# A two-layer SSD, attention and convolution trunk on one core: paired 128-column diagonal products, a padded decay contraction, dt weights side by side, and shorter chains in layer 0

## The chip, the cores and the metric

The kernel runs on one core of a Trainium2 chip. The metric is the device time of one execution in microseconds. The time before is 939.8 us, the median of three runs (937.92 to 940.81).

## The reference

The reference is a trunk of two layers on 512 tokens of width 1024, in float32. Each layer computes `x + RMSNorm_post(mixer(RMSNorm_pre(x)))`.

Layer 0 projects the normalised input once (`w_in`, 7200 columns) and splits it into gates `z`, an SSD branch (`xbc`, `dt`), and a forgetting-attention branch (`q`, `k`, `v`, `f`). The SSD branch is Mamba-2 in chunks of 128 tokens, with 16 heads of 64 columns in 4 groups:

```python
cs = jnp.cumsum(da, axis=2)                       # within a chunk of 128
decay = jnp.exp(jnp.where(causal, seg, -jnp.inf)) # seg[l, s] = cs[l] - cs[s]
cb = jnp.einsum('bclgn,bcsgn->bclsg', cc, bc)
y_diag = jnp.einsum('bclsgr,bcsgrp->bclgrp', cb[..., None] * decay, xd)
...
y_off = jnp.einsum('bclgn,bcgrpn->bclgrp', cc, h_in) * jnp.exp(cs)[..., None]
return (y_diag + y_off).reshape(bsz, s, g, r, p)
```

Its result is gated by `silu(z)`, normalised per group, joined with the gated output of the attention branch (16 heads, causal, with a decay in the logits), and multiplied by `w_out` (2048 x 1024). Layer 1 is a causal Conformer module: a projection to 6144 columns, a gated linear unit, a depthwise convolution of width 31, LayerNorm, a second gate, and an output projection (2048 x 1024).

## The kernel before

**Numbers in two parts.** Matmuls take float32 operands as two parts of the type fp32r: a high part (a cast on ScalarE, ACT) and the rest (a subtraction on VectorE, DVE, or GpSimd, POOL). A product is three matmuls (`mm3`, line 109): high by high, high by low, low by high. `hilo` (line 121) makes the two parts of a tile of 128 x 512.

**Jobs.** The weights come as a list of jobs of 512 KB each. Jobs 0 to 55 are layer 0's input projection, 56 to 71 (from `JO`) its output projection, and from 72 (`J1`) layer 1 follows. A job loads its weight block on SyncE's (SP's) queue, splits it in two parts, and runs in chunks; a chunk of a feature-major job is three matmuls of 512 columns. `z_ssd` (line 541) and `v_proj` (line 563) are token-major: they keep four, respectively two PSUM banks and walk over the k-tiles outside and the token blocks `b` inside. `out_proj` (line 632) has a first half of the columns (`first`, line 660) and a second (`second`, line 678); the last five jobs of the second half run together, block by block, and `finish` (line 707) ends each block: squares, the sum with the first half's `s0`, `var`, a power on POOL (`rstd_of`, line 344), and the residual. In layer 0, `done0` then takes the norm of layer 1 (`scaled`, line 358), and `start1` transposes the first two blocks (`uT`).

**The order of the work.** The order on TensorE (PE) is written out by hand; the other engines are ordered by the framework's scheduler, with priorities (`high_priority`). Between the chunks of the jobs, a planner (`Steps`, line 277) puts in the steps of SSD and attention, each when its needs are done and a due time has passed, by its own estimate of PE's time (`now`, in microseconds; `DL`, line 1236, holds the due times). The planner's steps for one SSD head are `seg` (line 1341: one matmul `bc` that spreads the cumulated decay over 128 partitions, contracting over 48 rows, and the exponential), `mprod` (line 1351) and `ydiag` (line 1356: per chunk one `mm3` of 64 columns). Per group come `states` (line 1299), `state_parts` (line 1316), `yoff` (line 1323), `gate` (line 1367), `gate_sums`, `gate_scale` and the transposes `to_yT` (line 1390). There are eight PSUM banks for everything. The diagonal products of a group's four heads share two banks, which `gate` reads.

**Residual weights prepared ahead.** `lo_ahead` (line 195) makes the low parts of layer 1's weights during layer 0: each step loads a block of 512 KB, casts it on ACT, subtracts on DVE (line 212), and stores the result to HBM. `run` (line 330) takes such a step every 8th chunk in jobs 5 to 12, every 7th from job 26, and every 11th from `JO` on, through the last job of layer 0.

**The start.** The four blocks of x are normalised (`scaled`) and transposed (`to_uT`, line 369), two blocks at a time. The first three jobs and the projection for `dt` and `f` run on half the tokens at a time (`together`, line 1129). The weights of `dt` and `f` lie in 48 columns (16, a gap, 16); their two parts are `dh` and `dl` (line 1105), and line 1156 takes the result from PSUM into `v`, from which the decay follows.

Of the kernel before, what the change touches and what calls it, by code (L numbers as in the profile page):

```python
# [15 lines left out]
P = 128  # L16
# [20 lines left out]
def trunk(  # L37
# [292 lines left out]
    def run(n, after=None):  # L330

        for _ in range(n):
            for c, _ in enumerate(chunks()):
                if after is not None:
                    after()
                i = state["run"]
                if 5 <= i < 13 or 26 <= i:
                    if (8 * i + c) % (11 if i >= JO else 7 if i >= 26 else 8) == 0:
                        next(early, None)
# [3 lines left out]

    def rstd_of(ss, n):
        v = col("var", ss.shape[-1])
        V.tensor_scalar(v, ss, 1.0 / n, EPS, ALU.mult, ALU.add)  # L346
        r = col("rstd", ss.shape[-1])
        mark["rstd"] = G.tensor_tensor(r, v, mhalf.to_broadcast([P, ss.shape[-1]]), ALU.pow).ins  # L348
        return r

    def sumsq(src, dst=None):
# [4 lines left out]
        return ss  # L356

    def scaled(dst, xs):

        s2 = col("s2", 2)  # L360
        for i, t in enumerate(xs):
            sumsq(t, s2[:, i : i + 1])
        if len(xs) == 2:
            V.tensor_tensor(s2[:, 0:1], s2[:, 0:1], s2[:, 1:2], ALU.add)
        r = rstd_of(s2[:, 0:1], D)
        for t, u in zip(xs, dst):
            mark["scale"] = V.tensor_scalar(u, t, r, None, ALU.mult).ins
# [173 lines left out]
    def z_ssd(ch):  # L541
        pbs = []

        def go(k2, wh, wl):
            if k2 == 0:
                pbs.extend(bank("tm") for _ in range(NB))
            for j in range(2):
                k = 2 * k2 + j
                for b in range(NB):
                    mm(pbs[b], uh[k][:, tok(b)], wh(j), k == 0, False)  # L550
                    mm(pbs[b], uh[k][:, tok(b)], wl(j), False, False)
                    mm(pbs[b], ul[k][:, tok(b)], wh(j), False, k == KT - 1)
# [10 lines left out]
    def v_proj(ch):  # L563
        pbs = []

        def go(k4, wh, wl):
            if k4 == 0:
                pbs.extend(bank("tm") for _ in range(2))
            for j in range(4):
                k = 4 * k4 + j  # L570
                for b in range(NB):
                    o = pbs[b // 2][:, b % 2 * 256 : b % 2 * 256 + 256]
# [59 lines left out]
    def out_proj(w, stages, nk, gpost, resid, done, hooks):  # L632
# [27 lines left out]
        def first(k2, wh, wl):  # L660
            if k2 == 0:
                pb0.extend(bank("o0") for _ in range(NB))
                if not at[-1]:
                    lead_in()
            for j in range(2):
                k = 2 * k2 + j
                for b in range(NB):
                    step(pb0[b], b, k, wh(j), wl(j))
                    if b < len(stages):
                        need(b, k + stages[b][1])  # L670
                    if k == nk - 1:
                        t = t2("o0")
                        s0.append(sumsq(pb0[b]))
                        V.tensor_tensor(t, pb0[b], gpost[0], ALU.mult)
# [32 lines left out]
        def finish(b):  # L707
            ss = sumsq(pb1[b])
            y1 = [o0[b], t2("y1")]
            V.tensor_tensor(y1[1], pb1[b], gpost[1], ALU.mult)  # L710
            V.tensor_tensor(ss, ss, s0[b], ALU.add)
            r = rstd_of(ss, D)
            for f in range(2):
# [390 lines left out]
    first = [bank("dtf"), bank("m"), bank("m"), bank("m")]  # L1104
    dh, dl = t2("dh", F32R)[:, : KT * 48], t2("dl", F32R)[:, : KT * 48]
    wdt = [lambda k, t=t: t[:, k * 48 : (k + 1) * 48] for t in (dh, dl)]
    us = [[xb[b][:, :S], xb[b][:, S:]] for b in range(NB)]
# [13 lines left out]
    to_uT(uh, ul, 0, us[0:2], c0, True)  # L1121
    split(dh, dl, raw[:, : KT * 48], A.copy, V)
# [4 lines left out]
    ws = [wdt] + [jobs[i].w for i in range(3)]  # L1127

    def together(js, half):

        gens = [fm_chunks(first[i], P if i else 48, *ws[i], uh, ul, slice(half * 256, half * 256 + 256)) for i in js]
        for _ in zip(*gens):
# [21 lines left out]
    with tc.high_priority(offset=HP):  # L1154
        v = row("v")
        V.tensor_scalar(v, pdt[:48, :], bcol, scol, ALU.add, ALU.mult)
        ab = row("ab")
# [45 lines left out]
    V.tensor_tensor(sel2, ident[0:48, 0:16], ident[0:48, 32:48], ALU.add)  # L1203
    tk = cp.tile([P, NB, P], F32, name="tk")
# [30 lines left out]
    SG = {}  # L1235
    DL = [2, 7, 4, 11, 4, 9, 4, 9, 9, 3, 3, 6]

# [16 lines left out]
    def x_tokens(g, i):  # L1254
# [44 lines left out]
    def states(g):  # L1299
# [6 lines left out]
        H = S_["H"] = [t2("H") for _ in range(2)]  # L1306
        for c in range(3):
            h = q256(H, c)
            if c == 0:
                A.copy(h, q256(st, 0))  # L1310
            else:
                dec = cdec[:, 4 * g : 4 * g + 4, c].unsqueeze(2).to_broadcast([P, 4, 64])
                V.tensor_tensor(h4(h), h4(q256(H, c - 1)), dec, ALU.mult)
                V.tensor_tensor(h, h, q256(st, c), ALU.add)

    def state_parts(g):
        H = SG[g]["H"]
        r = []
        for i, w in enumerate((512, 256)):
            r.append(hilo(H[i][:, :w], w))  # L1320
        SG[g]["H"] = [p[0] for p in r], [p[1] for p in r]

# [33 lines left out]
    def ydiag(h):  # L1356
        st = SG[h // 4]
        hh = h % 4
        if hh == 0:
            st["yd"] = [bank("yd") for _ in range(2)]  # L1360
        mh, ml = ms.pop(h)
        for c in range(NB):
            o = q256(st["yd"], c)[:, hh * 64 : hh * 64 + 64]
            xh, xl = [q256([p[i] for p in st["xd"]], c)[:, hh * 64 : hh * 64 + 64] for i in range(2)]
            mm3(o, mh[:, tok(c)], ml[:, tok(c)], xh, xl, True, True)

    def gate(g):
        with tc.high_priority(offset=HP):
            st = SG[g]
            y, yd = st["y"], st["yd"]  # L1370
            for i in range(2):
                V.tensor_tensor(y[i], y[i], yd[i], ALU.add)
                ys = y[i].rearrange("p (c f) -> p c f", c=2)
# [32 lines left out]
    def ssd(steps):  # L1406
        add = steps.add
        add("tk", decay_chain, ("dt", 24))
        for g in range(4):
# [10 lines left out]
            for h in range(4 * g, 4 * g + 4):  # L1420
# [16 lines left out]
            add(("gate", g), lambda g=g: gate(g), (("yd", 4 * g + 3), 0), (("yo", g), 0), (("silu", g // 2), 0), pe=False)  # L1437
            add(("gq", g), lambda g=g: gate_sums(g), (("gate", g), DL[9]), pe=False)
# [163 lines left out]
```

## Time and profile before

| | |
|---|---|
| median of three runs | 939.8 us |
| the profiled execution's own time | 940.86 us |
| its span, first to last instruction | 939.1 us |
| mean granted clock of PE | 0.993 |
| HBM read, written | 133.64 MB, 31.46 MB |
| DMA, mean over the span | 177 GB/s |
| layer 0, to layer 1's first matmul | 567.93 us |

The profile is of one execution. In a list of groups, a row gives the line, the engine, the operation, output and inputs by the program's names, the shape, the count, and after the bar the busy time in us, the mean of one in ns, and the engine's idle time before it. Most matmuls are made in one helper, so they all have line 102 (`mm`) or 106 (`tr`), and one tells them apart by the tile. Matmuls overlap: the distance from one start to the next says what one costs PE, not its own duration. In an order of time, a row gives the start in us, the duration, and in brackets the engine's idle time before it with what ended it. In a list of waits a row gives the waiting engine and tile, what released it, the us in total, the number of times and the longest. `PEld` is the loading of weights into PE, which runs beside the matmuls; `SPq` is the queue that issues the DMAs.

### The profile page before, as it was taken

What the parts mean: (1) busy time and instruction counts of PE and PEld (TensorE: products, weight loads), DVE (VectorE), ACT (ScalarE), POOL (GpSimd) and SP (SyncE); (2) the same over time, 40 slices, a digit from 0 to 9 for tenths busy, and PEclk for the clock granted to TensorE, in tenths of its full rate; (3) what the DMA queues carried; (4) which work ended last, traced back from release to release, by engine and by line L of the source; (5) the groups of instructions that cost most, each with busy time, mean ns of one, the idle gap of its engine ahead of it and who ended that gap; (6) DMA issues with size and microseconds to landing.
All of it is one profiled execution on the core that took longest, in us unless ns stands there. A gap on an engine that the chain in (4) does not pass through costs nothing.

```text
span 939.1 us, 13909 instructions
## 1 busy us (share of the span) xinstructions
PE 906.6 (97%) x4683; PEld 755.6 (80%) x4683; DVE 731.1 (78%) x1284; ACT 605.3 (64%) x1134; POOL 511.6 (54%) x476
## 2 busy tenths in 40 slices
PE   6999999998999999989899989999999999999997
PEld 6887787787798888778678879888888887787885
DVE  5667968788977887988877347899999999979502
ACT  5757667576855767677575536987886877658300
POOL 2604554535633444445573111998999999847310
PEclk9999999999999999999999999999999999999999
DMA  7725631347765574674538986546564665554503
GB/s 208 229 77 180 202 90 53 104 128 237 241 202 159 163 243 158 182 244 150 168 110 285 333 301 227 169 157 213 180 209 150 190 197 174 157 157 155 182 1 112
DMA packets 182507, 166.14 MB, mean 177 GB/s; under 512 B 7900, under 2 KB 151908, under 8 KB 182436
## 3 DMA queue, kind: packets, MB, share of 16 engines
q1 hardware_dynamic: 182420, 165.25, 54.9%
q8 instruction: 37, 0.61, 0.3%
q14 instruction: 34, 0.28, 0.1%
q10 hardware_dynamic: 16, 0.00, 0.0%
HBM read 133.64 MB, written 31.46 MB: 176 GB/s over the span
## 4 chain that ended last, share of the span: by engine, by line
PE 42%; DVE 6%; DMA 5%; issue 2%; ACT 2%; SPq 1%; POOL 1%; DVEq 0%; POOLq 0%; ACTq 0%
PE m L102 29%; PE o L102 10%; DMA lo<-pre 3%; DVE pre L212 2%; DMA wr<-in_o_w_in_dram 1%; PE acc L102 1%; PE tm L102 1%; DMA wr<-in_e_w_out_dram 1%; DVE w L191 1%; PE s L102 1%; DVE pl L119 1%; PE pT L106 0%; DMA pre<-in_o_w_in_dram 0%; ACT pr L95 0%; DMA pre<-in_o_w_out_dram 0%
## 5 line engine op out<-in xcount | busy, mean ns | idle before, releaser
L102 PE MATMUL m<-uh,w 128*128 128x512 f32 (+1 forms) x1392 | 453.5, 393 | 0.0
L102 PEld LDWEIGHTS m<-uh,w 128*128 128x128 f32 x1392 | 261.4, 190 | 50.9 <-issue 3.1
L102 PE MATMUL m<-ul,w 128*128 128x512 f32 (+1 forms) x696 | 267.7, 385 | 0.0
L191 POOL TENSOR_TENSOR w<-wr,w 128x512 fp32r<-128x512 f32 x112 | 158.8, 1442 | 160.3 <-ACT w L159 123.6
L984 DVE SCALAR_TENSOR_TENSOR acc<-h,cw,acc 128x490 f32<-128x490 f32 (+13 forms) x274 | 179.0, 731 | 2.7 <-ACT acc L976 2.0
L891 POOL TENSOR_TENSOR acc<-acc,prod 128x507 f32<-128x507 f32 (+9 forms) x124 | 159.6, 1289 | 8.2 <-ACT prod L877 0.7
L102 PEld LDWEIGHTS m<-ul,w 128*128 128x128 f32 x696 | 132.3, 190 | 21.5 <-issue 0.5
L102 PE MATMUL o<-w,hlh 128*128 128x512 f32 x448 | 142.2, 399 | 2.3 <-ACT pr L95 2.3
L212 DVE TENSOR_TENSOR pre<-pre,prh 128x512 fp32r<-128x512 f32 x104 | 90.6, 889 | 44.8 <-ACT prh L211 44.6
L102 PEld LDWEIGHTS o<-w,hlh 128*128 128x128 f32 x448 | 83.4, 191 | 19.0 <-ACT pr L95 3.0
L102 PE MATMUL tm<-w,uh 128*128 128x256 f32 (+1 forms) x384 | 91.7, 330 | 1.9 <-ACT pr L95 0.9
L211 ACT CAST prh<-pre 128x512 fp32r<-128x512 f32 x104 | 61.2, 622 | 48.5 <-DMA pre<-in_o_w_in_dram 14.6
L1464 POOL TENSOR_SCALAR pr<-pr,ri 128x128 f32<-128x128 f32 (+1 forms) x64 | 39.7, 621 | 92.6 <-DVE ri L1463 85.8
L159 ACT CAST w<-wr 128x1024 fp32r<-128x1024 f32 x72 | 74.8, 1048 | 23.0 <-DMA wr<-in_e_w_in_dram 6.6
L102 PE MATMUL o<-w,hll 128*128 128x512 f32 x224 | 88.0, 393 | 0.0
L877 ACT ACTIVATE prod<-h,cw 128x507 f32<-128x507 f32 (+9 forms) x124 | 79.0, 709 | 0.0
L348 POOL TENSOR_TENSOR rstd<-var,mhalf 128x1 f32<-128x1 f32 (+1 forms) x20 | 14.0, 698 | 114.6 <-DVE var L346 114.6
L157 ACT CAST w<-wr 128x1024 fp32r<-128x1024 f32 x56 | 57.2, 1050 | 18.5 <-DMA wr<-in_o_w_out_dram 10.3
L102 PEld LDWEIGHTS tm<-w,uh 128*128 128x128 f32 x384 | 62.9, 190 | 7.6 <-DVE QS L605 1.1
L102 PE MATMUL tm<-w,ul 128*128 128x256 f32 (+1 forms) x192 | 61.2, 319 | 0.0
L95 ACT ACTIVATE pr<-s,nmx 128x128 f32<-128x128 f32 (+1 forms) x64 | 34.0, 531 | 38.0 <-DVE nmx L1458 27.8
L102 PEld LDWEIGHTS o<-w,hll 128*128 128x128 f32 x224 | 42.6, 190 | 9.0
(270 smaller groups left out, 1594.3 us busy)
## 6 DMA issues: line engine op xcount, KB each, us to landing
wr<-in_e_w_in_dram SPq DMA_DIRECT2D x56, 512.0 KB
lo<-pre SPq DMA_DIRECT2D x52, 512.0 KB
pre<-in_o_w_in_dram SPq DMA_DIRECT2D x48, 512.0 KB
wr<-in_o_w_in_dram SPq DMA_DIRECT2D x48, 512.0 KB
w<-lo SPq DMA_DIRECT2D x48, 512.0 KB
wr<-in_e_w_out_dram SPq DMA_DIRECT2D x16, 512.0 KB
wr<-in_o_w_out_dram SPq DMA_DIRECT2D x16, 512.0 KB
x<-in_x_dram SPq DMA_DIRECT2D x12, 256.0 KB
```

The source lines that it names most:

```text
L95: i = A.activation(*a, **kw)
L102: T.matmul(o, l, r, start=start, stop=stop, skip_group_check=True)
L157: last_cast[0] = A.copy(hi, src).ins
L159: last_cast[0] = A.copy(hi, src).ins
L191: j.eng.tensor_tensor(hl[1][i][:, sl], src[:, sl], f32(hl[0][i])[:, sl], ALU.subtract)
L211: A.copy(h[:, sl], t[:, sl])
L212: V.tensor_tensor(t.bitcast(F32R)[:, sl], t[:, sl], f32(h)[:, sl], ALU.subtract)
L348: mark["rstd"] = G.tensor_tensor(r, v, mhalf.to_broadcast([P, ss.shape[-1]]), ALU.pow).ins
L877: A.activation(prs[i][:, s:], hs[j][:, : S - s], AF.Copy, scale=w31(30 - s, j))
L891: G.tensor_tensor(a2[j][:, s:], a2[j][:, s:], prs.pop(i)[:, s:], ALU.add)
L984: V.scalar_tensor_tensor(a[:, s:], h[:, : S - s], w31(30 - s, j), a[:, s:], ALU.mult, ALU.add)
L1464: G.tensor_scalar(p[:, :L], p[:, :L], ri, 1.0, ALU.mult, ALU.mult)
```

## The change

The change has eight parts, all but the second in layer 0 alone.

- `ydiag`: the two parts of x for a chunk lie side by side per head (`x_tokens` makes them so), and a head's chunk is one matmul of 128 columns (high of m by both parts of x) and one of 64 (low of m by high of x). The two parts of the result stand in PSUM beside each other, two banks now serve two heads, and a new step `yadd` adds them to y after each pair, with four additions on DVE.
- The norms: `var` is made by one operation from the second sum of squares and a term `pre` prepared from the first; in `finish` it stands ahead of the product `y1`. `out_proj` is shared with layer 1.
- `seg`: `cs2` and `sel2` have 128 rows in place of 48, the added ones zero.
- The dt weights: the low part stands at columns 64 to 111 beside the high part at 0 to 47. A matmul with 112 stationary columns and one with 48 replace three with 48. `v` is put together from both by two operations.
- `z_ssd`, `v_proj` and the first job of layer 0's output projection walk over the token blocks outside and the k-tiles inside.
- `states` and `state_parts` get high priority.
- The transposes `to_yT` are due 9 instead of 6 of the planner's microseconds after `gate_scale`.
- `lo_ahead`'s steps come at every 7th chunk from job 26 on, also in the output projection, and none in its last two jobs.

The diff, cut to its core:

```diff
-                if 5 <= i < 13 or 26 <= i:
-                    if (8 * i + c) % (11 if i >= JO else 7 if i >= 26 else 8) == 0:
+                if 5 <= i < 13 or 26 <= i < J1 - 2:
+                    if (8 * i + c) % (7 if i >= 26 else 8) == 0:
                         next(early, None)
...
-    def rstd_of(ss, n):
+    def rstd_of(ss, n, pre=None):
         v = col("var", ss.shape[-1])
-        V.tensor_scalar(v, ss, 1.0 / n, EPS, ALU.mult, ALU.add)
+        if pre is None:
+            V.tensor_scalar(v, ss, 1.0 / n, EPS, ALU.mult, ALU.add)
+        else:
+            V.scalar_tensor_tensor(v, ss, 1.0 / n, pre, ALU.mult, ALU.add)
...
+    def part_var(ss, n):
+
+        p = col("pre")
+        V.tensor_scalar(p, ss, 1.0 / n, EPS, ALU.mult, ALU.add)
+        return p
+
     def scaled(dst, xs):
 
-        s2 = col("s2", 2)
-        for i, t in enumerate(xs):
-            sumsq(t, s2[:, i : i + 1])
-        if len(xs) == 2:
-            V.tensor_tensor(s2[:, 0:1], s2[:, 0:1], s2[:, 1:2], ALU.add)
-        r = rstd_of(s2[:, 0:1], D)
+        pre = part_var(sumsq(xs[0]), D)
+        r = rstd_of(sumsq(xs[1]), D, pre)
...
-            for j in range(2):
-                k = 2 * k2 + j
-                for b in range(NB):
+            for b in range(NB):
+                for j in range(2):
+                    k = 2 * k2 + j
...
-            for j in range(4):
+            for b2 in range(2):
+              for j in range(4):
                 k = 4 * k4 + j
-                for b in range(NB):
+                for b in (2 * b2, 2 * b2 + 1):
...
+            stagger = k2 == 0 and len(stages) == 1
+            for j, b in ((j, b) for b in range(NB) for j in range(2)) if stagger else ((j, b) for j in range(2) for b in range(NB)):
...
             ss = sumsq(pb1[b])
+            r = rstd_of(ss, D, s0[b])
             y1 = [o0[b], t2("y1")]
             V.tensor_tensor(y1[1], pb1[b], gpost[1], ALU.mult)
-            V.tensor_tensor(ss, ss, s0[b], ALU.add)
-            r = rstd_of(ss, D)
...
+    dhl = [t2("dhl", F32R) for _ in range(2)]
+
+    def dt_parts():
+        for t in dhl:
+            G.memset(f32(t), 0.0)
+        for i, t in enumerate(dhl):
+            d4 = t.rearrange("p (k f) -> p k f", k=4)
+            s4 = raw[:, i * 192 : i * 192 + 192].rearrange("p (k f) -> p k f", k=4)
+            A.copy(d4[:, :, 0:48], s4)
+            V.tensor_tensor(d4[:, :, 64:112], s4, f32(d4[:, :, 0:48]), ALU.subtract)
+
+    def dt_chunks(sl):
+        for k in range(KT):
+            w = dhl[k // 4][:, k % 4 * P : k % 4 * P + 112]
+            mm(first[0][:112, sl], w, uh[k][:, sl], k == 0, False)
+            mm(first[0][:48, sl], w[:, :48], ul[k][:, sl], False, k == KT - 1)
+            yield
...
-        V.tensor_scalar(v, pdt[:48, :], bcol, scol, ALU.add, ALU.mult)
+        V.tensor_scalar(v, pdt[64:112, :], bcol, scol, ALU.add, ALU.mult)
+        V.scalar_tensor_tensor(v, pdt[:48, :], scol, v, ALU.mult, ALU.add)
...
-    cs2 = cp.tile([48, S], F32R, name="cs2")
-    sel2 = cp.tile([48, 16], F32R, name="sel2")
+    cs2 = cp.tile([P, S], F32R, name="cs2")
+    sel2 = cp.tile([P, 16], F32R, name="sel2")
...
-    DL = [2, 7, 4, 11, 4, 9, 4, 9, 9, 3, 3, 6]
+    DL = [2, 7, 4, 11, 4, 9, 4, 9, 9, 3, 3, 9]
...
-            st.setdefault("xd", []).append(hilo(pb))
+            xd = [t2("xd", F32R) for _ in range(2)]
+            src = pb.rearrange("p (c h f) -> p c h f", c=2, h=4)
+            parts = [t.rearrange("p (h t f) -> p h t f", h=4, t=2) for t in xd]
+            for c, t in enumerate(parts):
+                A.copy(t[:, :, 0, :], src[:, c])
+            for c, t in enumerate(parts):
+                V.tensor_tensor(t[:, :, 1, :], src[:, c], f32(t[:, :, 0, :]), ALU.subtract)
+            st.setdefault("xd", []).extend(xd)
...
-        mm(bc, sel2[:, h : h + 1].to_broadcast([48, P]), cs2, True, True)
+        mm(bc, sel2[:, h : h + 1].to_broadcast([P, P]), cs2, True, True)
...
-        if hh == 0:
+        if h % 2 == 0:
             st["yd"] = [bank("yd") for _ in range(2)]
         mh, ml = ms.pop(h)
         for c in range(NB):
-            o = q256(st["yd"], c)[:, hh * 64 : hh * 64 + 64]
-            xh, xl = [q256([p[i] for p in st["xd"]], c)[:, hh * 64 : hh * 64 + 64] for i in range(2)]
-            mm3(o, mh[:, tok(c)], ml[:, tok(c)], xh, xl, True, True)
+            o = q256(st["yd"], c)[:, h % 2 * P : h % 2 * P + P]
+            x = st["xd"][c][:, hh * P : hh * P + P]
+            mm(o, mh[:, tok(c)], x, True, False)
+            mm(o[:, :64], ml[:, tok(c)], x[:, :64], False, True)
+
+    def yadd(g, pair):
+
+        y, yd = SG[g]["y"], SG[g]["yd"]
+        with tc.high_priority(offset=HP):
+            for i in range(2):
+                ys = y[i].rearrange("p (c h f) -> p c h f", c=2, h=4)[:, :, 2 * pair : 2 * pair + 2, :]
+                parts = yd[i].rearrange("p (c h t f) -> p c h t f", c=2, h=2, t=2)
+                for t in range(2):
+                    V.tensor_tensor(ys, ys, parts[:, :, :, t, :], ALU.add)
...
-                V.tensor_tensor(y[i], y[i], yd[i], ALU.add)
...
+                if h % 2:
+                    add(("ya", h), lambda h=h: yadd(h // 4, h % 4 // 2), (("yd", h), 0), pe=False)
```

More of the change, by code (lines that the diff above doesn't have):

```diff
@@ L664, in first @@
                     lead_in()
-            for j in range(2):
-                k = 2 * k2 + j
-                for b in range(NB):
+            stagger = k2 == 0 and len(stages) == 1
+            for j, b in ((j, b) for b in range(NB) for j in range(2)) if stagger else ((j, b) for j in range(2) for b in range(NB)):
+                    k = 2 * k2 + j
                     step(pb0[b], b, k, wh(j), wl(j))
@@ L672, in first @@
                         t = t2("o0")
-                        s0.append(sumsq(pb0[b]))
+                        s0.append(part_var(sumsq(pb0[b]), D))
                         V.tensor_tensor(t, pb0[b], gpost[0], ALU.mult)
@@ L1104, in trunk @@
     first = [bank("dtf"), bank("m"), bank("m"), bank("m")]
-    dh, dl = t2("dh", F32R)[:, : KT * 48], t2("dl", F32R)[:, : KT * 48]
-    wdt = [lambda k, t=t: t[:, k * 48 : (k + 1) * 48] for t in (dh, dl)]
+    dhl = [t2("dhl", F32R) for _ in range(2)]
[13 more added lines that the diff above has]
+            yield
     us = [[xb[b][:, :S], xb[b][:, S:]] for b in range(NB)]
@@ L1121, in trunk @@
     to_uT(uh, ul, 0, us[0:2], c0, True)
-    split(dh, dl, raw[:, : KT * 48], A.copy, V)
+    dt_parts()
     for b in range(2, 4):
@@ L1126, in trunk @@
             split_to(b)
-    ws = [wdt] + [jobs[i].w for i in range(3)]
+    ws = [None] + [jobs[i].w for i in range(3)]
     def together(js, half):
-        gens = [fm_chunks(first[i], P if i else 48, *ws[i], uh, ul, slice(half * 256, half * 256 + 256)) for i in js]
+        sl = slice(half * 256, half * 256 + 256)
+        gens = [fm_chunks(first[i], P, *ws[i], uh, ul, sl) if i else dt_chunks(sl) for i in js]
         for _ in zip(*gens):
@@ L1202, in trunk @@
     V.tensor_copy(cs2[32:48, :], f32(csl)[0:16, :])
-    V.tensor_tensor(sel2, ident[0:48, 0:16], ident[0:48, 32:48], ALU.add)
+    V.tensor_tensor(sel2, ident[:, 0:16], ident[:, 32:48], ALU.add)
     tk = cp.tile([P, NB, P], F32, name="tk")
@@ L1305, in states @@
             mm3(q256(st, c), Bth[:, tok(c)], Btl[:, tok(c)], eh, el, True, True)
[L1306 to L1314, printed above, removed]
+        with tc.high_priority(offset=HP):
+            H = S_["H"] = [t2("H") for _ in range(2)]
+            for c in range(3):
+                h = q256(H, c)
+                if c == 0:
+                    A.copy(h, q256(st, 0))
+                else:
+                    dec = cdec[:, 4 * g : 4 * g + 4, c].unsqueeze(2).to_broadcast([P, 4, 64])
+                    V.tensor_tensor(h4(h), h4(q256(H, c - 1)), dec, ALU.mult)
+                    V.tensor_tensor(h, h, q256(st, c), ALU.add)
     def state_parts(g):
@@ L1318, in state_parts @@
         r = []
-        for i, w in enumerate((512, 256)):
-            r.append(hilo(H[i][:, :w], w))
+        with tc.high_priority(offset=HP):
+            for i, w in enumerate((512, 256)):
+                r.append(hilo(H[i][:, :w], w))
         SG[g]["H"] = [p[0] for p in r], [p[1] for p in r]
@@ L1362, in ydiag @@
         for c in range(NB):
-            o = q256(st["yd"], c)[:, hh * 64 : hh * 64 + 64]
-            xh, xl = [q256([p[i] for p in st["xd"]], c)[:, hh * 64 : hh * 64 + 64] for i in range(2)]
-            mm3(o, mh[:, tok(c)], ml[:, tok(c)], xh, xl, True, True)
+            o = q256(st["yd"], c)[:, h % 2 * P : h % 2 * P + P]
[4 more added lines that the diff above has]
+        y, yd = SG[g]["y"], SG[g]["yd"]
+        with tc.high_priority(offset=HP):
+            for i in range(2):
[3 more added lines that the diff above has]
+                    V.tensor_tensor(ys, ys, parts[:, :, :, t, :], ALU.add)
     def gate(g):
@@ L1369, in gate @@
             st = SG[g]
-            y, yd = st["y"], st["yd"]
+            y = st["y"]
             for i in range(2):
-                V.tensor_tensor(y[i], y[i], yd[i], ALU.add)
                 ys = y[i].rearrange("p (c f) -> p c f", c=2)
@@ L1434, in ssd @@
                 add(("yd", h), lambda h=h: ydiag(h), *need)
+                if h % 2:
+                    add(("ya", h), lambda h=h: yadd(h // 4, h % 4 // 2), (("yd", h), 0), pe=False)
                 if h % 4 == 1:
                     add(("yo", g), lambda g=g: yoff(g), (("hp", g), DL[8]))
-            add(("gate", g), lambda g=g: gate(g), (("yd", 4 * g + 3), 0), (("yo", g), 0), (("silu", g // 2), 0), pe=False)
+            add(("gate", g), lambda g=g: gate(g), (("ya", 4 * g + 3), 0), (("yo", g), 0), (("silu", g // 2), 0), pe=False)
             add(("gq", g), lambda g=g: gate_sums(g), (("gate", g), DL[9]), pe=False)
```

## Prediction

> **What bounds the kernel now.** I read the page first, then the list of waits for the matmul engine, then busy time by stretches, and last the order of time around each edited place.
>
> ```profile
> span 939.1 us, 13909 instructions
> PE 906.6 (97%) x4683; PEld 755.6 (80%) x4683; DVE 731.1 (78%) x1284; ACT 605.3 (64%) x1134; POOL 511.6 (54%) x476
> ```
>
> PE is busy for 97% of the span, so time is won only by taking matmuls off PE or by ending one of its few waits. The list of waits names those (us in total, times, longest):
>
> ```profile
> PE uT L106 <- DVE x L367: 6.1, 3, 3.7
> PE uT L106 <- DVE u L367: 2.8, 1, 2.8
> PE yT L106 <- DVE y L1388: 2.6, 2, 1.6
> PE o L102 <- ACT pr L95: 2.5, 4, 0.9
> ...
> PE yo L102 <- DVE hll L119: 2.0, 2, 1.6
> ...
> PE tm L102 <- ACT pr L95: 0.9, 1, 0.9
> PE tm L102 <- DVE QS L605: 0.9, 1, 0.9
> ```
>
> Busy time in three stretches (columns PE, PEld, DVE, ACT, POOL, clock, DMA share, GB/s): one of layer 1, the whole SSD stage of layer 0, and its tightest part.
>
> ```profile
> 650.00:675.00 25.00, 25.00 (x112) 20.72 (x111) 25.00 (x40) 21.12 (x34) 24.06 (x20) 1.00 0.55 180
> 70.00:290.00 220.00, 215.40 (x1148) 178.07 (x1147) 179.48 (x294) 145.60 (x254) 110.94 (x84) 0.99 0.54 164
> 90.00:120.00 30.00, 27.96 (x154) 23.94 (x154) 29.31 (x45) 19.77 (x38) 14.89 (x9) 1.00 0.58 176
> ```
>
> In layer 1 PE never stops. The diff takes nothing out of it but the end of each output block, so layer 1 should move earlier as a whole. In the SSD stage PE is busy 98% and DVE 82%, but from 90 to 120 us DVE is busy 29.31 of 30. DVE is the engine that can take back what PE wins.
>
> **The diagonal products.** A `yd` matmul today has 64 columns; each of 16 heads has 4 chunks of 3. The change makes it 2 per chunk, one of 128 columns and one of 64.
>
> ```profile
> L102 PE MATMUL yd<-hlh,hll 128*128 128x64 f32 x64 | 17.7, 277 | 0.0
> ```
> ```profile
> 100.13 0.28 PE L102 MATMUL yd<-hll,hlh 128*128 128x64 f32 x1
> ...
> 101.24 0.28 PE L102 MATMUL yd<-hlh,hll 128*128 128x64 f32 x1
> ```
> ```profile
> 81.48 0.28 PE L102 MATMUL cb<-hll,hlh 128*128 128x128 f32 x1
> ...
> 82.60 0.28 PE L102 MATMUL cb<-hlh,hll 128*128 128x128 f32 x1
> ```
>
> The first row is one of three groups of 64, so there are 192 matmuls, and the change drops 64. What counts is the distance between starts, not the 277 ns of one. From 100.13 to 101.24 lie ten steps: 0.111 us each with 64 columns. From 81.48 to 82.60 lie ten steps with 128 columns: 0.112 us. The wider matmul costs what the narrow one does, so 64 x 0.111 = **7.1 us** goes from PE.
>
> The Trainium skill, page "TensorE: Matmul & The Clock Gate", section "Back-to-back issue gap", speaks against this edit: its table gives about 60 cycles up to 64 columns and 134 for 128. By that, 192 x 60 = 11,520 cycles become 64 x 134 + 64 x 60 = 12,416, which is 0.4 us more at the page's 2.4 GHz, and the net sum below would be 12.4 us instead of 19.9. The `cb` rows disagree with it here.
>
> **The decay matmul.** `bc` contracts over 48 rows; the change pads it to 128.
>
> ```profile
> 85.25 0.40 PE L102 MATMUL tm<-w,ul 128*128 128x512 f32 x1
> 85.58 0.49 PE L102 MATMUL bc<-cs,sel 48*128 48x512 f32 x1
> 86.00 0.73 PE L102 MATMUL tm<-w,uh 128*128 128x512 f32 x2
> 86.57 0.39 PE L102 MATMUL tm<-w,ul 128*128 128x512 f32 x1
> 86.80 0.63 PE L102 MATMUL tm<-w,uh 128*128 128x512 f32 x2
> ```
> ```profile
> 294.00 0.28 PE L102 MATMUL s<-KS,QS 128*128 128x256 f32 x1
> 294.12 0.28 PE L102 MATMUL s<-KX,QX 68*128 68x256 f32 x1
> ```
>
> Between ordinary 512-column matmuls a step is 86.80 - 86.57 = 0.23 us. The matmul ahead of `bc` and `bc` itself take 86.00 - 85.25 = 0.75 us, that is 0.29 more than two steps. A contraction over 68 rows follows its neighbour after 0.12 us, so it is not partial rows as such, but 48 of them, that cost. I take the extra as gone: 16 heads x 0.29 = **4.6 us**; the bounds are 0 and 4.6.
>
> The Trainium skill, page "TensorEngine Tiling (Array Packing)", section "Theoretical Speedup", promises up to twice the speed for a small dimension of 64 or less; by it padding forgoes something, and the sum would lack this 4.6 us. The rows show the short one 0.29 us dearer.
>
> **The dt weights.** 48 matmuls of 256 columns become 32.
>
> ```profile
> 33.17 0.28 PE L102 MATMUL dtf<-uh,dh 128*48 128x256 f32 x1
> 33.28 0.28 PE L102 MATMUL dtf<-ul,dh 128*48 128x256 f32 x1
> ```
> ```profile
> 17.35 1.22 DVE L191 TENSOR_TENSOR w<-wr,w 128x1024 fp32r<-128x1024 f32 x1
> ```
> ```profile
> 18.39 0.28 PE L102 MATMUL m<-uh,w 128*128 128x256 f32 x1
> ...
> 28.33 0.32 PE L102 MATMUL dtf<-ul,dh 128*48 128x256 f32 x1 [0.16 <-DVE ul L399]
> ```
>
> Sixteen at about 0.115 us are 1.8 us. But the eight of the first half end at 18.39, just as the residual weights for the next job come from DVE (17.35 + 1.22 = 18.57), and at 28.33 PE waits for `ul` anyway. What is saved before that turns into waiting. Only the eight after it count: **0.9 us** (bounds 0 and 1.8). The two memsets, the second cast and subtraction, and the second operation on `v` lie beside this: POOL is 54% busy, and the `bc` rows above, which need the decay, stand at 85 us. If that cover fails, the 0.9 is gone.
>
> **Waits at the head of a step.** High priority for `states` and `state_parts` aims at the 2.0 us of `yo`; the same DVE work must still be done in the 98% busy stretch, so I count **1.5**. The later due time of `yT` (9 instead of 6 of the planner's microseconds) is longer than either of its waits (longest 1.6), while the gate's chain grows by about 0.3 through narrower additions: **2.0** of 2.6. Going through one bank after the other in `z_ssd`, `v_proj` and the first output job asks for the second bank later and frees the first one sooner. That speaks to the `o` and `tm` waits, 4.3 us together; the softmax exponentials behind them are not faster, so I count about half, **2.0** (bounds 0 and 4.3).
>
> **The preparation of layer 1's residual weights** moves forward within the output projection and leaves its last job.
>
> ```profile
> 552.16 0.15 DVE L711 TENSOR_TENSOR ss<-ss,ss 128x1 f32<-128x1 f32 x1
> 557.05 0.69 DVE L212 TENSOR_TENSOR pre<-pre,prh 128x512 fp32r<-128x512 f32 x1 [4.75 <-ACT prh L211]
> 557.66 0.15 DVE L346 TENSOR_SCALAR var<-ss 128x1 f32<-128x1 f32 x1
> ```
>
> The sum of squares of the second block is added at 552.3, but the next link, `var`, runs at 557.66, because DVE stands in order behind a `pre` subtraction that waits 4.75 us for its cast (and that for its load). This 5 us delay is what PE pays for with the 2.8 us of `uT` <- `u`. With no such step in the last job the chain is ready ahead of PE: **2.8 us**. What moves with it is every load, cast, subtraction and store of those steps, and SP's queue carries them among the weight loads:
>
> ```profile
> 525.00:560.00 35.00, 34.86 (x155) 28.63 (x153) 10.48 (x22) 11.34 (x24) 4.84 (x5) 1.00 0.92 314
> ```
> ```profile
> pre<-in_o_w_in_dram SPq DMA_DIRECT2D x48, 512.0 KB
> ```
>
> A step loads and stores 512 KB each way. Seven chunks of three matmuls at 0.23 us last 4.8 us, so the steps ask for about 217 GB/s, and one output weight of 512 KB in eight chunks (5.5 us) for 95 more: 312 GB/s, which is what the DMA carried at 92% (314). It just fits, and the output weights are loaded well ahead. I price it at nothing, with up to 4 us as the bound if loads come late.
>
> **The chains.** In the RMS norms one operation leaves the chain, and in `finish` the product `y1` goes behind `var`:
>
> ```profile
> 933.03 0.69 DVE L710 TENSOR_TENSOR y<-o,x 128x512 f32<-128x512 f32 x1 [3.75 <-ACT junk L355]
> ...
> 933.82 0.15 DVE L346 TENSOR_SCALAR var<-ss 128x1 f32<-128x1 f32 x1
> ```
>
> After the last matmul `var` can run at 933.03 in place of 933.82; the product hides under the power on POOL: **0.8 us**. At the start the same cut is one short operation per block, **0.2 us** of the 6.1.
>
> **What it adds to DVE.** 32 additions of 256 elements replace 8 of 512, and 16 half-width subtractions replace 8 in `x_tokens`.
>
> ```profile
> 99.63 0.42 DVE L1314 TENSOR_TENSOR H<-H,st 128x256 f32<-128x256 f32 x1
> ```
> ```profile
> L1372 DVE TENSOR_TENSOR y<-y,yd x8: 680/680/681, 115.1 to 273.4; 128x512 f32<-128x512 f32 x8
> ```
>
> 32 x 0.42 - 8 x 0.68 = 8.0, and 16 x 0.42 - 8 x 0.68 = 1.3: 9.3 us in a stage in which DVE has 40 us free, but not evenly (the casts that are halved with them are on ACT, 64% busy). I let a fifth reach PE, **2.0 us** (bounds 0 and 9.3).
>
> **Sum.** 7.1 + 4.6 + 0.9 + 1.5 + 2.0 + 2.0 + 2.8 + 0.8 + 0.2 = 21.9, less 2.0: **19.9 us**. The profiled execution took 940.86 us with a span of 939.1, a microsecond above the median of 939.8; from the median the forecast is **919.9 us**.
>
> **The rivals.**
> - *The other engines hold the pace.* PE runs ahead by 12.6 us of matmuls, but DVE from 90 to 120 us, and the exponentials behind `o` and `tm`, do not get faster; all 9.3 us of new DVE work and none of the `yo`, `yT`, `o` and `tm` gains (5.5) show: 19.9 - 7.3 - 5.5 = 7.1, or 932.7; halfway there is 926.3. For it: 29.31 of 30. Against: 82% over the stage. Chance 0.17 for between 924 and 933.
> - *Columns set the price.* If a 128-column matmul takes twice 0.111, 64 x 0.222 + 64 x 0.111 equals today's 192 x 0.111, and the 7.1 us are not there: 927.0. The table of the Trainium skill quoted above would have it so; `cb` at 0.112 speaks against. Chance 0.04.
> - *The edit of `bc` does not do what it says.* Its stationary operand stays a column repeated 128 times; if that repetition, not the 48 rows, costs the 0.29, nothing changes: 924.5. Chance 0.07.
> - *All the waits go,* with the other half of dt: 19.9 + 2.0 + 0.5 + 0.6 + 2.3 + 0.9 gives 26.2, or 913.6. Chance 0.10.
> - *Slower.* The additions of a pair run at high priority and DVE is in order. If they stand, unfinished matmuls ahead of them, in front of the next two heads' products and subtractions (four passes of 512 at about 0.68), PE waits for 4 x 0.42 + 4 x 0.68 = 4.4 us after each of eight pairs: 35 us against 21.9, so 953. It turns from gain to loss above 2.7 us a pair. Against it: no `yd` wait stands in the list today, and the planner asks for a head's product 9 us ahead. Chance 0.04, with 0.03 for a milder form that ends within 0.3%.
>
> **How the numbers follow.** The forecast with its own range, 915 to 925, has 0.55. The range of 8 in 10 takes in the case of all waits below and most of the first rival above: 912 to 929. Smaller than 0.3%, some 2.8 us, a measurement of this kernel cannot tell from no change. Faster 0.93, same 0.03, slower 0.04.
>
> **What would show it.** PE's matmuls fall from 4683 by 80 to 4603. `yd` starts stay 0.11 us apart with 128 columns; the steps around `bc` become 0.23; `uT` <- `u` and `yo` leave the list of waits; `var` follows the last square at once. Layer 1 from its first `m` to the last `o` keeps its length. I am wrong if the 128-column starts are 0.2 apart, if new waits of PE for DVE stand between 90 and 280 us, or if `o` waits for weight loads near 500.

## The result, and the profile after

The changed kernel takes 929.2 us in the median (927.4 to 930.1) against 939.85 before: a ratio of 0.9882, with a 95% interval of 0.9858 to 0.9907. It is 10.6 us faster. The forecast was 919.9 us; the measured median lies outside its own range (915 to 925) and 0.2 us above the upper end of the range of 8 in 10 (912 to 929). The direction held; nearly half of the gain is missing.

The page after begins with these lines:

```profile
span 927.6 us, 13837 instructions
PE 892.8 (96%) x4603; PEld 748.1 (81%) x4603; DVE 740.6 (80%) x1318; ACT 604.5 (65%) x1143; POOL 520.6 (56%) x478
```

PE has the 80 matmuls fewer that the prediction counted. The work came off as foreseen. This is the order of time on PE around two decay matmuls, and in one head's diagonal products:

```profile
83.02 0.40 PE L102 MATMUL tm<-w,ul 128*128 128x512 f32 x1
83.25 0.39 PE L102 MATMUL bc<-cs,sel 128*128 128x512 f32 x1
83.48 0.62 PE L102 MATMUL tm<-w,uh 128*128 128x512 f32 x2
83.93 0.39 PE L102 MATMUL tm<-w,ul 128*128 128x512 f32 x1
...
99.30 0.31 PE L102 MATMUL yd<-xd,hlh 128*128 128x128 f32 x1
99.44 0.25 PE L102 MATMUL yd<-xd,hll 128*128 128x64 f32 x1
99.52 0.31 PE L102 MATMUL yd<-xd,hlh 128*128 128x128 f32 x1
```

Every step around `bc` is now 0.23 us. A pair of one 128-column and one 64-column matmul takes 99.52 - 99.30 = 0.22 us: 0.14 from the wide one to the next start and 0.08 from the narrow one, 0.11 on average, as the `cb` rows of before had it. The three narrow ones of before took 0.33.

The list of PE's waits after shows where the rest went (us in total, times, longest):

```profile
PE uT L106 <- DVE x L372: 5.5, 2, 3.7
PE xt L106 <- ACT cv L95: 4.0, 1, 4.0
...
PE s L102 <- ACT pr L95: 2.2, 2, 1.8
PE yd L102 <- DVE hll L119: 1.9, 2, 1.0
PE yT L106 <- DVE y L1431: 1.5, 2, 0.9
PE s L102 <- DVE os L1536: 1.5, 2, 1.0
PE pT L106 <- ACT pr L95: 1.1, 2, 0.8
...
PE m L102 <- ACT yT L1441: 1.0, 1, 1.0
```

`uT` <- `u` and `yo` <- `hll` have left the list, as predicted (a wait of `yo` for `cv`, 0.4 us, is new). But `xt` (4.0), `yd` (1.9) and `m` <- `yT` (1.0) are new, and the `s` and `pT` waits for the softmax are longer.

The same can be summed. Below is PE's busy time from the start to layer 1's first matmul, from the busy time by stretches (columns: length, PE, PEld, DVE, ACT, POOL, clock, DMA share, GB/s), before and after:

```profile
0.00:567.90 567.90, 543.52 (x2987) 453.88 (x2988) 428.71 (x772) 365.21 (x722) 248.04 (x255) 0.99 0.59 186
```
```profile
0.00:557.60 557.60, 529.76 (x2908) 446.57 (x2909) 437.46 (x804) 363.86 (x730) 255.92 (x257) 0.99 0.61 193
```

PE's busy time fell by 13.8 us, and its idle time rose from 24.4 to 27.8 us. Layer 0 became 10.3 us shorter. DVE's busy time rose by 8.8 us; the prediction had counted 9.3.

The largest new wait is read in four rows. Before, three of the four operations in which DVE scales the third group's gated y took 0.88 us together (the fourth, later, 0.70). After, DVE has the rows of the second list there, and ACT and PE follow:

```profile
222.49 0.88 DVE L1388 TENSOR_SCALAR y<-y,rstd 128x256 f32<-128x256 f32 x3 [0.24 <-POOL rstd L348]
```
```profile
216.12 5.25 DVE L1431 TENSOR_SCALAR y<-y,rstd 128x256 f32<-128x256 f32 x4 [0.41 <-POOL rstd L351]
221.29 3.45 DVE L212 TENSOR_TENSOR pre<-pre,prh 128x512 fp32r<-128x512 f32 x2
224.66 2.31 DVE L533 SCALAR_TENSOR_TENSOR cv<-m,c,cv 128x511 f32<-128x511 f32 x3
```
```profile
227.06 0.63 ACT L95 ACTIVATE cv<-cv 128x512 f32<-128x512 f32 x1 [1.15 <-DVE cv L533]
```
```profile
227.74 0.90 PE L106 MATMUL xt<-ident,cv 128*128 128x128 f32 x3 [4.04 <-ACT cv L95]
```

One operation of the same shape takes 1.31 us instead of 0.29, and the subtraction of residual weights 1.73 instead of 0.68. Behind them stands the convolution `cv` that the transpose `xt` needs. The same six microseconds by stretches, before and after (POOL is the fifth engine: 3.38 and 6.00 us), with POOL's own rows after:

```profile
216.00:222.00 6.00, 5.38 (x24) 4.13 (x22) 6.00 (x10) 3.58 (x12) 3.38 (x3) 1.00 0.85 264
```
```profile
216.00:222.00 6.00, 4.46 (x21) 3.40 (x20) 5.88 (x5) 3.85 (x7) 6.00 (x6) 1.00 0.53 161
226.00:234.00 8.00, 6.26 (x21) 5.13 (x22) 3.48 (x7) 5.08 (x9) 2.51 (x2) 0.57 0.99 310
```
```profile
216.05 2.60 POOL L191 TENSOR_TENSOR w<-wr,w 128x512 fp32r<-128x512 f32 x2
218.62 1.34 POOL L119 TENSOR_TENSOR hll<-cv,hlh 128x512 fp32r<-128x512 f32 x1
219.91 2.60 POOL L191 TENSOR_TENSOR w<-wr,w 128x512 fp32r<-128x512 f32 x2
```

After, POOL works all through the stretch, and DVE's five operations fill it. The Trainium skill, page "SBUF — State Buffer", section "SBUF: two separate sides", says that VectorE and GpSimd share a pair of ports as an exclusive lock, which an operation that needs it holds to its end. These rows agree with it: POOL's operations take 1.30 us each, and beside them a scaling takes 1.31 us and not 0.29. Slow scalings are not new. Before, the sixteen of layer 0 took 0.34 us at least, 0.69 in the median and 1.39 at most; after, 0.34, 1.37 and 1.39. The third group's now fall into a stretch in which POOL works.

PE's row from 226 to 234 us shows what follows: a granted clock of 0.57 of full speed. The kernel before is at half speed in this place too, for 3.4 us from 225.8 on, behind its `yT` waits; after the change it is 6.8 us (226.9 to 233.7). Over the whole of layer 0 the two profiled executions have the same 10.2 us at half speed (before from 225.8, 457.9 and 563.7 us, 3.4 each; after 6.8 from 226.9 and 3.4 from 404.4), so the clock does not explain the missing gain.

### The profile page after: what moved, and what is told of

It is laid out like the page before. It is cut to its first block, busy times and chain, and to the rows that moved or that the text cites. A ratio compares the mean times of both kernels' runs of the same rounds, so it can differ in the third digit from the quotient of the medians.

```text
span 927.6 us, 13837 instructions
## 1 busy us (share of the span) xinstructions
PE 892.8 (96%) x4603; PEld 748.1 (81%) x4603; DVE 740.6 (80%) x1318; ACT 604.5 (65%) x1143; POOL 520.6 (56%) x478
## 4 chain that ended last, share of the span: by engine, by line
PE 64%; DVE 14%; ACT 7%; issue 6%; DMA 4%; POOL 3%; SPq 0%; DVEq 0%; POOLq 0%; ACTq 0%
PE m L102 37%; PE o L102 18%; PE tm L102 4%; DVE pre L212 3%; POOL w L191 2%; ACT w L159 1%; DMA lo<-pre 1%; DMA pre<-in_o_w_in_dram 1%; PE s L102 1%; PE pT L106 1%; DVE cv L533 1%; DVE y L1431 1%; DVE seg L1380 1%; DVE pl L119 1%; DVE w L191 1%
## 5 line engine op out<-in xcount | busy, mean ns | idle before, releaser
L191 POOL TENSOR_TENSOR w<-wr,w 128x512 fp32r<-128x512 f32 x112 | 168.1, 1526 | 148.3 <-ACT w L159 112.3
L102 PE MATMUL o<-w,hlh 128*128 128x512 f32 x448 | 140.2, 394 | 0.8 <-ACT pr L95 0.8
L102 PEld LDWEIGHTS o<-w,hll 128*128 128x128 f32 x224 | 42.0, 188 | 10.3 <-POOL hll L119 0.9
```

What stands on the lines that cost most here:

```text
L102: T.matmul(o, l, r, start=start, stop=stop, skip_group_check=True)
L191: j.eng.tensor_tensor(hl[1][i][:, sl], src[:, sl], f32(hl[0][i])[:, sl], ALU.subtract)
```

## The experiments

Twelve kernels ran. Times are medians, ratios are to the kernel before on the same chip, and idle is the length of the stretch to layer 1's first matmul less PE's busy time in it. Ratios, not medians, are compared across chips. The last three columns are of one profiled execution each.

| run | us | ratio, 95% interval | to layer 1 | PE busy | PE idle |
|---|---|---|---|---|---|
| before | 939.85 | 1 | 567.9 | 543.5 | 24.4 |
| changed | 929.2 | 0.9882 (0.9858-0.9907) | 557.6 | 529.8 | 27.8 |
| u_diag | 931.4 | 0.9917 (0.9902-0.9932) | 558.6 | 534.7 | 23.9 |
| u_decay | 928.4 | 0.9890 (0.9874-0.9907) | 556.3 | 532.1 | 24.2 |
| u_pace | 931.0 | 0.9913 (0.9898-0.9928) | | | |
| e29 | 928.9 | 0.9896 (0.9882-0.9911) | | | |
| nopre | 904.3 | 0.9604 (0.9589-0.9619) | 532.5 | 520.7 | 11.8 |
| u_yprio | 928.1 | 0.9864 (0.9840-0.9887) | | | |
| e_gact | 925.2 | 0.9827 (0.9806-0.9847) | 553.7 | 527.9 | 25.8 |
| u_both | 934.2 | 0.9915 (0.9883-0.9946) | | | |
| n_before | 919.1 | 0.9769 (0.9754-0.9784) | 545.6 | 534.9 | 10.7 |
| n_diag | 910.6 | 0.9679 (0.9661-0.9697) | 538.7 | 527.7 | 11.0 |
| n_decay | 910.7 | 0.9680 (0.9664-0.9695) | 539.1 | 527.3 | 11.8 |
| e_mix | 923.3 | 0.9820 (0.9799-0.9841) | 551.5 | 527.6 | 23.9 |

### One part undone: the diagonal products, the decay matmul, the pace

`u_diag` puts `ydiag`, the layout of x and the addition in `gate` back:

```diff
-            mm(o, mh[:, tok(c)], x, True, False)
-            mm(o[:, :64], ml[:, tok(c)], x[:, :64], False, True)
+            mm3(o, mh[:, tok(c)], ml[:, tok(c)], xh, xl, True, True)
```

> The changed kernel with the diagonal products, the layout of x and the addition to y as before; everything else stays changed. Theory 1 (the matmuls taken off PE are won; what is missing of the forecast was lost in one place, near 216 to 240 us, where a pile of work on DVE makes a transpose of x wait): the 64 matmuls of 0.111 us come back, so about 7 us slower than the changed kernel, 936, or somewhat less if the pile near 216 us changes as well. Theory 2 (the extra additions on DVE cost what the diagonal products win): no slower than the changed kernel, 929 or below.

`u_decay` puts 48 rows back:

```diff
-        mm(bc, sel2[:, h : h + 1].to_broadcast([P, P]), cs2, True, True)
+        mm(bc, sel2[:, h : h + 1].to_broadcast([48, P]), cs2, True, True)
```

> The changed kernel with the decay matmul over 48 rows again. Theory 1: the gaps of 0.29 us around each of 16 matmuls come back, 4.6 us, about 934. Rival (the repeated column of the stationary operand, not the 48 rows, made the gap, and the gain is elsewhere): 929, and the gap is the same in both traces.

`u_pace` puts the pace of the residual weights back:

```diff
-                if 5 <= i < 13 or 26 <= i < J1 - 2:
-                    if (8 * i + c) % (7 if i >= 26 else 8) == 0:
+                if 5 <= i < 13 or 26 <= i:
+                    if (8 * i + c) % (11 if i >= JO else 7 if i >= 26 else 8) == 0:
```

> The changed kernel with the preparation of layer 1's residual weights paced as before: every 11th chunk in the output projection, through the last job. Theory 1: the wait of uT for u comes back with about 3 us, 932 to 933. Rival (the quicker pace costs the output projection elsewhere, through DMA and DVE, what it saves there): 929 or below.

Without the new diagonal products the ratio is 0.0035 higher, about 3 us of 940 and not 7, with intervals that still touch. PE's work came back (4.9 us more busy), but 3.9 us of idle time left with it. Most of that is the wait of `xt`, 0.8 us here and 4.0 in the changed kernel: the pile near 216 us changed as well, which theory 1 had allowed for. Without the padded decay matmul no loss is seen (0.0008, within the intervals), although its trace shows the gaps of before:

```profile
86.11 0.39 PE L102 MATMUL tm<-w,ul 128*128 128x512 f32 x1
86.43 0.49 PE L102 MATMUL bc<-cs,sel 48*128 48x512 f32 x1
86.85 0.73 PE L102 MATMUL tm<-w,uh 128*128 128x512 f32 x2
87.42 0.40 PE L102 MATMUL tm<-w,ul 128*128 128x512 f32 x1
```

So it is not the repeated column that costs. The gap is there, and so is its price on PE, yet PE's idle time is 3.6 us less than in the changed kernel. The clock of the one execution has a part in the missing loss: layer 0 was at half speed for 3.4 us here and for 10.2 in the changed kernel, which makes PE's work some 3.4 us shorter. Whether the padding gains anything is settled only by `n_decay` below. The pace is the one part that behaved as theory 1 said: about 3 us slower without it, though the intervals touch, with this wait in the list again:

```profile
PE uT L106 <- DVE u L372: 2.2, 1, 2.2
```

Theory 1 called for one lost place. Two parts whose matmuls are worth little each, with idle time that moves the other way, speak for something that gives matmul time back wherever it is won, but they do not settle it.

### The pile at 216 us taken apart

`e29` starts the second stretch of residual weights at job 29 and paces it by 6:

```diff
-                if 5 <= i < 13 or 26 <= i < J1 - 2:
-                    if (8 * i + c) % (7 if i >= 26 else 8) == 0:
+                if 5 <= i < 13 or 29 <= i < J1 - 2:
+                    if (8 * i + c) % (6 if i >= 29 else 8) == 0:
```

> The changed kernel with the second stretch of that preparation begun at job 29 instead of 26 and paced at every 6th chunk, so that no such step stands on DVE near 205 to 230 us. Theory 1: the transpose of x no longer waits 4 us there, the half-speed window of PE after it is at least halved, and about 5 us are won: 923 to 925. Theory 2 (the pile is the additions and the gate themselves): the wait stays, 929.

Neither theory was right. The `xt` wait fell from 4.0 to 1.2 us, so the pile did contain the preparation, but the time did not move. At 245 us the matmuls of the jobs were 13.4 us ahead of the same ones of the kernel before; then `yd` waited for DVE (1.07 us at 248.25 and 1.36 at 251.74) and PE ran at half speed for some 10 us, as the granted clock in the second row shows, and at 262 us the lead was 8.4:

```profile
240.00:250.00 10.00, 8.93 (x77) 8.78 (x75) 9.39 (x17) 9.97 (x17) 3.94 (x3) 1.00 0.50 157
250.00:261.00 11.00, 9.64 (x50) 9.56 (x49) 10.21 (x17) 5.84 (x11) 5.33 (x4) 0.53 0.52 166
```

So part of what the shorter wait gave went to the clock: the mean granted clock of this kernel's four executions is 0.987 to 0.994, that of the changed kernel's 0.992 to 0.997.

### The load of DVE taken away

Theory 1 was given up for theory 3: in layer 0, DVE sets the pace at the places where PE waits. `nopre` leaves out the subtraction of the residual weights:

```diff
-                V.tensor_tensor(t.bitcast(F32R)[:, sl], t[:, sl], f32(h)[:, sl], ALU.subtract)
```

> The changed kernel without one part of the computation: the DVE subtraction that makes layer 1's residual weights during layer 0 is left out (104 operations, 92 us of DVE), so that layer 1 multiplies by wrong low parts at the same cost. Its loads, casts and stores stay. Theory 3 (in layer 0 DVE sets the pace at the places where PE waits, so matmuls taken off PE come back as waits): PE's waits up to layer 1's first matmul fall from 29.7 us to about 20, and the time to 915 to 919. Rival (the waits come from chains of other engines and from the order of the steps, not from DVE's load): waits stay above 27, 926 to 930.

(The 29.7 us in this text are sums over the distances between matmuls; the table's 27.8 are PE's idle time, which is the measure used here.) This is the largest effect of the study: 0.9604 against 0.9882, about 26 us, and more than theory 3 had forecast (915 to 919 us). Its row and the first waits of its list:

```profile
0.00:532.50 532.50, 520.69 (x2908) 442.84 (x2909) 357.60 (x700) 364.98 (x730) 240.19 (x257) 1.00 0.64 202
```
```profile
PE uT L106 <- DVE x L371: 5.1, 2, 3.9
PE pv L106 <- POOL keep L441: 3.1, 1, 3.1
PE dtf L102 <- DVE ul L403: 0.9, 1, 0.9
PE o L102 <- DVE hll L119: 0.7, 1, 0.7
```

With 80 us less on DVE, PE's idle time in layer 0 falls by 16 us, and 9.6 of the 11.8 us left lie in the first 40 us. PE is also busy 9 us less with the same matmuls, and the granted clock is 1.00: no stretch at half speed is left in layer 0. The 10.2 us at half speed of the changed kernel account for about 5 of these 9 us; where the other 4 come from is not shown.

The three runs that follow repeat comparisons from above without this load. `n_decay` and `n_diag` are `u_decay` and `u_diag`, and `n_before` is the kernel before, each with the same line left out.

> The changed kernel without the DVE subtraction of the residual weights (so layer 1 has wrong low parts, as in the run nopre) and with the decay matmul over 48 rows. With that subtraction in place this edit was worth nothing (928.4 against 929.2). Theory 3 (DVE's load gives the saved matmul time back as waits): without that load the 16 gaps of 0.29 us show in full, 904.3 + 4.6 = 908.9. Rival (the gap is hidden under something else whatever DVE does): 904 to 905.

> The changed kernel without the same subtraction (wrong low parts in layer 1) and with the diagonal products as before. With the subtraction in place this edit was worth 2.1 us. Theory 3: without it the 64 matmuls of 0.111 us show in full, 904.3 + 7.1 = 911.4. Rival (the additions cost on PE what they cost before, whatever the load): 906 to 907.

> The kernel before without the same subtraction (wrong low parts in layer 1). Theory 3: of the prediction's 21.9 us the matmuls (12.6) and the chains (1.0) remain, while the waits that the change aims at are gone in both kernels: about 904.3 + 14.5 = 918.8. Rival (the change's worth does not depend on DVE's load): 904.3 + 10.6 = 914.9.

All three came out on theory 3's side. Against `nopre`, undoing the diagonal products costs 0.0075, or 7.1 us, where 7.1 was worked out; with the load it was 3. Undoing the decay padding costs 0.0076, also about 7 us, where 4.6 was expected and the load had left nothing to be seen. The whole change is worth 0.0165, or 15.5 us, where 14.5 was expected (the two terms named there, 12.6 and 1.0, make 13.6). With the load in place it is worth 0.0118, or 11.1 us by the ratio. The 4.4 us between the two are more than the intervals leave to chance (about 3). Most of what the load costs has nothing to do with the change: leaving the line out is worth 0.0231, about 22 us, in the kernel before and 26 in the changed one. Row of `n_before`:

```profile
0.00:545.60 545.60, 534.87 (x2987) 449.41 (x2988) 346.09 (x664) 364.51 (x721) 232.95 (x255) 1.00 0.62 195
```

Here the change takes 14.2 us off PE (534.87 to 520.69), and the idle time rises by only 1.1 us (10.7 to 11.8). Whether it is the subtraction's busy time that counts, its place in the queue, or what it costs POOL (whose busy time in layer 0 falls by 15.7 us from the changed kernel to `nopre`) can't be told from these runs: leaving the operation out ends all three.

### The scheduling edits

`u_yprio` runs the additions at ordinary priority, `u_both` undoes the priority of `states` and `state_parts` and the due time of `yT`:

```diff
-        with tc.high_priority(offset=HP):
+        if True:
...
-    DL = [2, 7, 4, 11, 4, 9, 4, 9, 9, 3, 3, 9]
+    DL = [2, 7, 4, 11, 4, 9, 4, 9, 9, 3, 3, 6]
```

> The changed kernel with the additions of the diagonal products at ordinary priority on DVE. Theory 3 with the additions as its cause: the yd waits for DVE (2.6 us) go, 926 to 927. Rival (the place of the additions does not matter): the same within 1 us, 929.

> The changed kernel with two of its scheduling edits undone: states and state_parts at ordinary priority, and the transposes of y due 6 instead of 9. The prediction's steps for these (1.5 and 2.0 us): the waits of yo and yT for DVE come back, 932 to 933. Theory 3 (the waits only change their place): 929 within 1.5 us.

The place of the additions makes no difference beyond the intervals (0.9864 and 0.9882 overlap), and the `yd` waits for DVE stay: 1.9 for `hll` and 0.7 for `H` in the changed kernel, 2.6 and 0.3 here. Undoing the two scheduling edits makes the kernel about 3 us slower by the ratio, but the intervals overlap; the four executions lie between 929.4 and 935.6. In the profiled one the loss is not in `yo` or `yT`, as the prediction had it, but in a wait of `yd` for the states' recurrence, and in a half-speed stretch around it:

```profile
PE yd L102 <- DVE H L1346: 6.5, 1, 6.5
```
```profile
196.00:214.00 18.00, 11.53 (x44) 9.87 (x44) 15.55 (x26) 7.50 (x14) 5.48 (x4) 0.62 0.68 204
```

### Two versions that relieve DVE

`e_gact` moves the scaling of the gated y to ACT. `e_mix` does the same and takes the first eight steps of the residual weights out of the first group's stage:

```diff
-                V.tensor_scalar(q256(y, c), q256(y, c), r[:, c : c + 1], None, ALU.mult)
+                A.activation(q256(y, c), q256(y, c), AF.Copy, scale=r[:, c : c + 1])
...
-                if 5 <= i < 13 or 26 <= i < J1 - 2:
-                    if (8 * i + c) % (7 if i >= 26 else 8) == 0:
+                if 3 <= i < 9 or 26 <= i < J1 - 2:
+                    if (8 * i + c) % (7 if i >= 26 else 6) == 0:
```

> The changed kernel with the scaling of the gated y (four operations a group) moved from DVE to ACT. In the changed kernel four of them take 5.25 us on DVE at 216 us while POOL works, ahead of the convolution that the transpose of x waits for. Theory 3: that wait of 4.0 us and part of the half-speed window behind it go, 923 to 925. Rival (the wait is made by the preparation of the residual weights, which stands there too): 928 to 930.

> The changed kernel with the scaling of the gated y on ACT and the first eight steps of the residual weights in jobs 3 to 8 (every 6th chunk) in place of jobs 5 to 12 (every 8th), where DVE is idle half of the time, and out of the stage of the first group of heads. Theory 3: the yd and yo waits near 100 us (about 2 us) go, 922 to 924. Rival: only the place of the waits changes, 925 as with the scaling alone.

Both are faster than the changed kernel: 0.9827 and 0.9820, against 0.9882, with intervals that do not meet its own. Sixteen operations moved off DVE are worth about 5 us. The wait of `xt` fell as theory 3 said, from 4.0 us to 0.6 in `e_gact`, but PE is still at half speed there for 6.8 us, from 234.0 on. Between the two the difference is within the intervals, although the `yd` waits of 1.9 us are gone from the list of `e_mix`, so its rival stands. A large new wait stands in both. In `e_mix` it reads so, on PE and on ACT:

```profile
234.57 0.80 PE L102 MATMUL m<-uh,w 128*128 128x512 f32 x1 [4.92 <-ACT zf L600]
```
```profile
232.90 1.14 ACT L211 CAST prh<-pre 128x512 fp32r<-128x512 f32 x2 [5.08 <-DMA pre<-in_o_w_in_dram]
233.94 0.58 ACT L600 COPY zf<-m 128x512 f32<-128x512 f32 x1
```

These rows show ACT in order as well: the cast of a residual weight waits 5.08 us for its load, and the copy that frees PE's bank stands behind it.

## Why the prediction was right and wrong

- **The bound: right for work, wrong for waits.** "Time is won only by taking matmuls off PE or by ending one of its few waits" held, but the waits were taken as separate items that can be ended one by one. PE's busy time fell by 13.8 us and its idle time rose by 3.4, where the forecast had 12.6 and a fall of about 6.3 (8.3 from the heads of steps and `uT`, 2.0 back). This step failed, and it is the whole miss: the idle time came out some 9.7 us longer than forecast. The clause "DVE is the engine that can take back what PE wins" named the right engine, but its price was a fifth of 9.3 us. The runs show that the change is worth 4.4 us more when DVE is relieved (15.5 against 11.1). That the other 5 us or so went the same way is argued from the lists of waits and not shown, since without the load the waits that the edits aimed at are gone from both kernels. One of the prediction's own signs of being wrong came true: new waits of PE for DVE between 90 and 280 us (`yd` at 102.6, 106.0 and 256.2).
- **The diagonal products: right.** The 7.1 us show in full when DVE is relieved (7 by the ratio, give or take 2), and about 3 of them with DVE as it is. The table of the Trainium skill quoted in the prediction does not fit these rows, since a pair of 128 and 64 columns takes 0.22 us, like two of 64.
- **The decay matmul: mechanism right, size too small.** The rival of the repeated column is out: it is still there and the gap is gone. The price was read from one distance too few. In the rows of before, the two steps from 86.00 to 86.57 take 0.57 us and not 0.46, so the step after `bc` pays another 0.11: 0.40 x 16 = 6.4 us, above the prediction's upper bound of 4.6 and near the 7.1 (0.0076) that the runs show. The speedup table of the Trainium skill that the prediction sets against this is about several small tiles that work side by side in the array; `bc` runs alone, so no run here tests it.
- **The dt weights.** The wait of `dtf` for `ul` grew from 0.2 to 0.9 us, as foreseen. No run isolates the 0.9 us of the rest.
- **`yo` and `yT`: wrong in kind.** `yo` <- `hll` left the list, but `yd` waits for `hll` in the same stretch, and `yT` still waits 1.5 us. Undoing both edits costs about 3 us, if anything (the intervals overlap), through a wait that the trace of before does not contain.
- **`tm` and `o`: 2.0 was too much.** `o` <- `pr` fell from 2.5 to 0.8 us and `tm` <- `pr` from 0.9 to 0.3, but `s` and `pT` waits for the softmax grew by about as much: 1.5 to 2.2, 0.7 to 1.5, and 1.1 for `pT`. It looks as if the block order had moved the wait to the next consumer, but no run undid it alone.
- **The preparation moved forward: right.** The 2.8 us are gone, and 2.2 come back with the old pace. No wait of `o` for weight loads appeared. The price left something out: right behind that wait the kernel before was at half speed for 3.4 us (granted clock 0.50), and `u_pace` is again (from 553.1 on), while the changed kernel is not.

```profile
563.70:567.10 3.40, 3.40 (x13) 2.92 (x12) 3.40 (x9) 3.06 (x9) 0.00 (x0) 0.50 0.92 297
```

- **The chains: right.** `var` now runs first, and the last block's scaling begins 0.89 us after it:

```profile
922.35 0.16 DVE L349 SCALAR_TENSOR_TENSOR var<-ss,pre 128x1 f32<-128x1 f32 x1 [4.51 <-ACT junk L358]
922.43 0.68 DVE L717 TENSOR_TENSOR y<-o,x 128x512 f32<-128x512 f32 x1
923.24 0.75 DVE L719 SCALAR_TENSOR_TENSOR o<-o,rstd,x 128x512 f32<-128x512 f32 x1
```

From the start of the last matmul to the end it was 7.3 us before (931.84 to 939.1) and is 6.4 after (921.21 to 927.6). The span fell by 11.5 us and layer 0 by 10.3; this tail is most of the difference. Layer 1 from its first `m` to its last `o` kept its length (363.9 and 363.7 us).

- **The range.** Of the rivals, the first one ("the other engines hold the pace") is nearest to what happened; halfway into it stood 926.3, and the result is 929.2. With DVE busy 29.31 of 30 us in the rows of before, its chance of 0.17 was too small.

## What to carry to other kernels

When one engine is busy 97% of the time, its few waits still show which other engine sets the pace at those places, and work taken off the first can come back there as new waits. Before pricing such an edit, take the load off the second engine in an experiment, even if that leaves part of the computation out: `nopre` and `n_before` separate what an edit removes from what the schedule returns. And look for background work that stands in order in the queues of the engines on the path, since it costs its waits as well as its operations.

## What the runs showed of the hardware that was not expected

- A contraction over 48 rows between 128-row matmuls costs 0.40 us beyond its own length, in three pieces: before, in and after it. One over 68 rows costs nothing: with 256 columns it starts 0.12 us after its neighbour (294.00 to 294.12), as 128-row ones of that width do.
- DVE operations stretch to 2.5 to 4.5 times their length while POOL works: 0.29 to 1.31 us for a scaling of 256 columns, 0.68 to 1.73 for a subtraction of 512.
- PE falls to half speed after short waits among small matmuls. In `e29` PE was busy 8.93 of the 10 us ahead of its slow stretch (0.53 from 250 to 261 us), and 2.33 of the last 3.4:

```profile
246.90:250.30 3.40, 2.33 (x20) 2.14 (x19) 3.12 (x6) 3.40 (x7) 0.79 (x1) 0.99 0.80 287
```

The Trainium skill, page "TensorE: Matmul & The Clock Gate", section "Part 1: The HAM clock gate", describes the slow state as following an idle window of about 3.4 us; here 1.1 us of idle time within it was enough. In `nopre`, without the waits, no such stretch is left in layer 0.
